# Two FFN layers with seven block products in place of eight, and the modulation vectors moved to the first layer

## The chip, the cores and the metric

The kernel runs on one core of one Trainium2 chip. The metric is the device time of one execution in microseconds (us); the time shown is the median of the runs.

## The reference

Two streams, 512 latent tokens and 256 context tokens of width 1024, pass through two layers. Each layer is a half FFN, a mixer, and a second half FFN. The mixer of the first layer (Fourier group and gated linear attention) is called even here, that of the second (short convolution and differential attention) odd. Every part has a normed input with a shift and a scale, and a gate on what it adds; these come from the conditioning vector of the stream.

```python
def _modulation(cond, w, b):
    m = jax.nn.silu(cond) @ w + b
    return jnp.split(m[..., None, :], N_MOD, axis=-1)

def _prenorm(h, gain, shift, scale):
    return _rmsnorm(h, gain) * (1.0 + scale) + shift

def _swiglu(h, w_in, w_out):
    g, u = jnp.split(h @ w_in, 2, axis=-1)
    return (jax.nn.silu(g) * u) @ w_out
...
        h = h + 0.5 * g1 * _swiglu(_prenorm(h, norm_ffn1[layer], sh1, sc1), ffn1_w_in[layer], ffn1_w_out[layer])
        hc = hc + 0.5 * cg1 * _swiglu(_prenorm(hc, norm_ffn1[layer], csh1, csc1), ffn1_w_in[layer], ffn1_w_out[layer])
```

The hidden width is 2816. There are nine modulation vectors for each layer and stream.

## The kernel before, in words

Activations lie transposed: 8 chunks of 128 features, each with the tokens along the free axis, and a token's normed input is h * gain * (1 + scale); the factor 1/rms of a token is multiplied in after the product (`scaled`, L305), and two extra columns hold the shifts of the two streams, so that one product gives tokens and shifts. To come near to float32, each operand is split into a high part (ScalarE's copy, `split_w` L164, `split` L145) and a low part (VectorE's difference, L165, L146), and each product is three matmuls (`mm3`, L248): high by high, high by low, low by high.

An FFN layer (`ffn`, L677) takes the 22 chunks of 128 hidden columns in four groups (6, 6, 6, 4). For a chunk it loads the weights of gate and up (1024 x 128 each, 512 KB) on SP's queue, splits them, and multiplies them with the two token halves, context (256, with the shifts 258 columns) and latent (512): 2 weights x 8 feature chunks x 3 matmuls, for each half. VectorE and ScalarE make the hidden chunk `hh`, `hl` from the sums. After a group, `out_phase` (L611) multiplies its hidden chunks with the output weights, 8 output chunks for each half, and adds the gated sum to the residual stream (`hlat`, `hctx`, L627). In front of the first layer come its own shift and scale.

The other modulation vectors are made on VectorE (`mod_tile`, L477): a tile of 128 outputs is loaded (`ada`, 512 KB on SP's queue) and for each stream one instruction multiplies it with the conditioning vector and adds up (`junk`, L484). A group of eight tiles is one vector. These tiles are dealt out evenly over the hidden chunks of a layer, from chunk 3 on: 48 tiles of two streams in the first FFN layer, 48 of two streams in the second, 32 of one stream in the third.

The order of instructions on each engine is set when the program is built, by a scheduler that takes the program's order as priority; every engine then takes its own list in that order. Pools of buffers decide when a tile can be written: 3 raw weights (`wraw`), 4 split weights (`wsp`), 7 hidden chunks, 4 modulation tiles in the first layer, 7 PSUM banks for sums (6 in the first layer).

## Time and profile before

| | us |
|---|---|
| device time, median of 3 runs | 2778.92 |
| lowest and highest run | 2778.41 and 2778.99 |
| span of the profiled execution, first to last instruction | 2776.5 |
| device time of the profiled execution itself | not recorded |
| TensorE busy | 2722.8 (98%) |
| VectorE busy | 1751.6 (63%) |
| ScalarE busy | 986.2 (36%) |
| GpSimd busy | 236.0 (9%) |

Busy time is the time in which at least one instruction of the engine runs; rows of one engine overlap, so that the sum of their lengths is more. DVE is VectorE, ACT ScalarE, PE TensorE, POOL GpSimd, SP the queue of the plain transfers. The layers follow one another: the first FFN layer to about 534 us, the even mixer to about 940, the second FFN layer to 1490, the third to 1985, the odd mixer to about 2390, then the last.

### The profile page before, as it was taken

The page shows a single profiled execution, that of the slowest core. Times are in us where ns is not written, and L with a number is a line of the kernel's source. Part 1 is how long each engine was busy: PE and PEld are TensorE (multiplying, and loading weights), DVE is VectorE, ACT ScalarE, POOL GpSimd, SP SyncE. Part 2 cuts the span into 40 slices and gives each one's busy share as a digit, 9 for nine tenths or more (in the row PEclk, how much of TensorE's full clock was granted, in tenths as well). Part 3 has the DMA queues.
Part 4 walks back from the last instruction along what each step waited for, and adds up shares of the span by engine and source line. Part 5 has one row for each costly group of instructions (what it writes and reads, how often), then busy time and mean ns, then how long its engine had stood idle before and what let it go on. Part 6 is the DMA issues. An engine that isn't in the chain of part 4 may idle for free.

```text
span 2776.5 us, 42228 instructions
## 1 busy us (share of the span) xinstructions
PE 2722.8 (98%) x17198; PEld 2425.7 (87%) x17198; DVE 1751.6 (63%) x3181; ACT 986.2 (36%) x1628; POOL 236.0 (9%) x231
## 2 busy tenths in 40 slices
PE   9999999999999999999999999999999999999998
PEld 7888888888888888888888888888888888999997
DVE  6647475678889764747566445454478888744545
ACT  4312121255544621212125212121256666522323
POOL 2000000030000200000002000000052223100002
PEclk9999999999999999999999999999999999999999
DMA  7324333312111132324332323233222212222221
GB/s 260 130 90 131 105 131 110 109 63 69 54 58 54 69 116 98 132 95 137 107 122 76 101 97 105 86 101 105 92 77 61 73 57 75 76 98 87 95 96 61
DMA packets 87554, 267.84 MB, mean 96 GB/s; under 512 B 10736, under 2 KB 18256, under 8 KB 87360
## 3 DMA queue, kind: packets, MB, share of 16 engines
q1 hardware_dynamic: 83248, 255.08, 27.4%
q0 software_dynamic: 3024, 9.01, 1.3%
q8 instruction: 136, 2.23, 0.3%
q10 hardware_dynamic: 1088, 1.05, 0.1%
q14 instruction: 58, 0.48, 0.1%
HBM read 255.14 MB, written 2.10 MB: 93 GB/s over the span
## 4 chain that ended last, share of the span: by engine, by line
PE 83%; DVE 11%; ACT 3%; issue 2%; DMA 1%; POOL 0%; SPq 0%; DVEq 0%; ACTq 0%; POOLq 0%
PE mm L170 81%; DVE al L602 1%; DVE mx L1245 1%; DVE gS L1046 1%; DVE hlat L627 1%; PE sc L170 1%; DVE wl L165 1%; ACT e L1247 1%; ACT wh L164 1%; PE n L170 0%; DVE hctx L627 0%; PE mm L177 0%; ACT ah L601 0%; DVE atl L146 0%; DVE e L1259 0%
## 5 line engine op out<-in xcount | busy, mean ns | idle before, releaser
L170 PE MATMUL mm<-ah,wh 128*128 128x258 f32 (+2 forms) x3536 | 1163.6, 329 | 7.4 <-DVE t L308 4.6
L170 PE MATMUL mm<-al,wh 128*128 128x258 f32 (+2 forms) x3536 | 1149.1, 325 | 0.0
L170 PE MATMUL mm<-ah,wl 128*128 128x258 f32 (+2 forms) x3536 | 1147.4, 324 | 1.6 <-DVE wl L165 1.6
L170 PEld LDWEIGHTS mm<-ah,wh 128*128 128x128 f32 x3536 | 669.2, 189 | 71.8 <-DVE t L308 4.2
L170 PEld LDWEIGHTS mm<-ah,wl 128*128 128x128 f32 x3536 | 669.2, 189 | 59.5 <-DVE wl L165 1.8
L170 PEld LDWEIGHTS mm<-al,wh 128*128 128x128 f32 x3536 | 670.2, 190 | 55.6 <-issue 1.4
L164 ACT ACTIVATE wh<-wr 128x1024 fp32r<-128x1024 f32 (+2 forms) x361 | 354.4, 982 | 934.5 <-PE mm L170 834.2
L170 PE MATMUL mm<-hh,wh 128*128 128x256 f32 (+1 forms) x1408 | 454.3, 323 | 0.0
L170 PE MATMUL mm<-hl,wh 128*128 128x256 f32 (+1 forms) x1408 | 453.3, 322 | 0.0
L170 PE MATMUL mm<-hh,wl 128*128 128x256 f32 (+1 forms) x1408 | 453.3, 322 | 0.0
L308 DVE TENSOR_TENSOR t<-mm,R 128x256 f32<-128x256 f32 (+2 forms) x376 | 195.1, 520 | 362.5 <-PE mm L170 362.1
L165 DVE TENSOR_TENSOR wl<-wr,wh 128x1024 fp32r<-128x1024 f32 (+2 forms) x325 | 371.1, 1142 | 47.8 <-ACT wh L164 43.5
L627 DVE SCALAR_TENSOR_TENSOR hlat<-mm,mod,hlat 128x512 f32<-128x512 f32 (+1 forms) x216 | 139.4, 649 | 277.2 <-PE mm L170 276.8
L170 PEld LDWEIGHTS mm<-hh,wl 128*128 128x128 f32 x1408 | 265.8, 189 | 23.5
L170 PEld LDWEIGHTS mm<-hl,wh 128*128 128x128 f32 x1408 | 264.5, 188 | 23.9
L170 PEld LDWEIGHTS mm<-hh,wh 128*128 128x128 f32 x1408 | 264.4, 188 | 23.9
L484 DVE SCALAR_TENSOR_TENSOR junk<-ada,cond 128x1024 bf16<-128x1024 f32 x224 | 273.8, 1222 | 2.8 <-DMA ada<-in_adaT_dram 2.3
L536 POOL TENSOR_TENSOR nacc<-nacc,nsq 128x256 f32<-128x256 f32 x47 | 39.5, 841 | 1973.9 <-ACT nsq L532 1945.2
L711 ACT ACTIVATE t<-t,c 128x256 f32<-128x256 f32 (+1 forms) x176 | 103.2, 586 | 247.4 <-DVE t L308 241.0
L145 ACT ACTIVATE hh<-t 128x256 fp32r<-128x256 f32 (+1 forms) x176 | 87.6, 498 | 280.9 <-DVE t L713 279.4
L713 DVE SCALAR_TENSOR_TENSOR t<-t,c,t 128x256 f32<-128x256 f32 (+1 forms) x176 | 102.7, 584 | 19.9 <-ACT t L711 4.7
L146 DVE TENSOR_TENSOR hl<-t,hh 128x256 fp32r<-128x256 f32 (+1 forms) x176 | 91.7, 521 | 35.2 <-ACT hh L145 35.0
(275 smaller groups left out, 2256.9 us busy)
## 6 DMA issues: line engine op xcount, KB each, us to landing
wr<-in_ffn_in_dram SPq DMA_DIRECT2D x176, 512.0 KB, 3.5
ada<-in_adaT_dram SPq DMA_DIRECT2D x128, 512.0 KB, 3.4
wr<-in_ffn_out_dram SPq DMA_DIRECT2D x96, 384.0 KB, 3.1
wr<-in_odd_w_dram SPq DMA_DIRECT2D x24, 512.0 KB, 3.5
wr<-in_even_w_dram SPq DMA_DIRECT2D x21, 512.0 KB, 3.5
wn<-in_ada_dram SPq DMA_DIRECT2D x16, 512.0 KB, 5.2
wr<-in_ffn_out_dram SPq DMA_DIRECT2D x16, 512.0 KB, 3.6
wr<-in_mix_out_dram SPq DMA_DIRECT2D x16, 256.0 KB, 2.6
```

The costliest lines, as they stand in the source:

```text
L145: self.nc.scalar.activation(hi, src, AF.Copy)
L146: self.nc.vector.tensor_tensor(lo, src, hi.bitcast(F32), op=ALU.subtract)
L164: self.nc.scalar.activation(hi, rv, AF.Copy)
L165: self.wl_engine.tensor_tensor(lo, rv, hi.bitcast(F32), op=ALU.subtract)
L170: i = self.nc.tensor.matmul(*a, **k)
L308: self.nc.vector.tensor_tensor(dst, ps, self.R[:ps.shape[0], hf[0]:hf[1]], op=ALU.mult)
L484: nc.vector.scalar_tensor_tensor(junk, w, 1.0, self.cond[:, s, :], op0=ALU.mult, op1=ALU.mult, accum_out=self.mods[l][:, s, n:n + 1]))
L536: self.acc_engine.tensor_tensor(acc[:, :w], acc[:, :w], sq[:, :w], op=ALU.add)
L602: nc.vector.scalar_tensor_tensor(lo[:, a], self.hv(k, s0, s1), G, hi[:, a].bitcast(F32), op0=ALU.mult, op1=ALU.subtract)
L627: nc.vector.scalar_tensor_tensor(hv, ps[:, s0 - t0:s1 - t0], gate, hv, op0=ALU.mult, op1=ALU.add)
L711: nc.scalar.activation(sg, sg, AF.Silu, bias=c[0][:, st:st + 1])
L713: nc.vector.scalar_tensor_tensor(sg, su, c[1][:, st:st + 1], sg, op0=ALU.add, op1=ALU.mult)
```

## The change

In the second and third FFN layer, chunks 2 to 21 are made by `ffn_fast`. A chunk's in-projection is seen as a 2 x 2 block product: the weights by gate and up and by the two halves of the features, the activations by the two halves of the features and of 772 columns (768 tokens and four columns of shifts), 386 each. Strassen's scheme in Winograd's form replaces the eight block products by seven, with sums of weight blocks and of activation blocks as operands, each product of 4 feature chunks x 3 matmuls x 386 columns.

- `sums_of_acts` makes the activation sums once in a layer: ScalarE writes unsplit activations into two buffers (`sg`), VectorE combines them, and they are split.
- The weight sums are made in part by transfers: SP loads a block of 256 KB into a buffer `sg`, and a transfer on GpSimd's queue adds the other block to it (`half_sum`, `SUM`). VectorE adds the rest (`prep`).
- The products of a chunk share PSUM banks; ScalarE copies partial sums out (`p1`, `p3`, `p5`), VectorE combines (`p6`, `p2`, `p7`, `p4`). TensorE takes the products of these layers in the order of the program.
- The groups are 2, 4, 4, 4, 4 and 4 chunks; 4 buffers for hidden chunks in place of 7.
- Modulation vectors: 96 tiles of two streams and 24 of one are computed in the first FFN layer (216 instructions, before 96), none in the second and third, and one vector (8 tiles of one stream) in the last; they are dealt out over chunks and over the units of the output phases (`pace`).

```diff
+    def sums_of_acts(self, l, gsh, gsc, tp):
+        nc = self.nc
+        TA, T3 = [], []
+        for kp in range(4):
+            b = []
+            for k in (kp, kp + 4):
+                x = self.sg.tile([P, 1024], F32, tag="sg", name=self.nm("bt"))[:, :TOK + 4]
+                for c0, c1, st in self.segs(0, TOK):
+                    nc.scalar.activation(x[:, c0:c1], self.hv(k, c0, c1), AF.Copy,
+                                         scale=self.mods[l][:, st, 8 * gsc + k:8 * gsc + k + 1])
+                S = self.mods[l][:, 0:2, 8 * gsh + k].unsqueeze(1).to_broadcast([P, 2, 2])
+                nc.scalar.activation(x[:, TOK:].rearrange("p (a b) -> p a b", b=2), S, AF.Copy)
+                b += [x[:, :HALF], x[:, HALF:]]
+            t = self.tmpt(TOK + 4)
+            t1, t2 = t[:, :HALF], t[:, HALF:]
+            nc.vector.tensor_tensor(t1, b[0], b[1], op=ALU.subtract)
+            nc.vector.scalar_tensor_tensor(t2, t1, -1.0, b[3], op0=ALU.mult, op1=ALU.subtract)
+            TA.append(tuple(tp.tile([P, TOK + 4], F32R, name=self.nm(n)) for n in ("tah", "tal")))
+            self.split(*TA[-1], t)
+            u = self.tmpt(TOK + 4)
+            t3, t4 = u[:, :HALF], u[:, HALF:]
+            nc.vector.tensor_tensor(t3, b[3], b[1], op=ALU.subtract)
+            nc.vector.scalar_tensor_tensor(t4, t2, -1.0, b[2], op0=ALU.mult, op1=ALU.subtract)
+            T3.append(tuple(tp.tile([P, HALF], F32R, name=self.nm(n)) for n in ("t3h", "t3l")))
+            self.split(*T3[-1], t3)
+            self.split(*(x[:, HALF:] for x in self.A[kp]), t4)
...
+    def ffn_fast(self, l, w_in, w_out, gate, gsh, gsc, halves, last):
+        nc, a = self.nc, self.a
+        win = a[w_in][l]
+        hid = self.hidden(l, w_in, [0, 1], halves)
+        with ExitStack() as es:
+            tp = es.enter_context(self.tc.tile_pool(name=self.nm("tp"), bufs=1))
+            rhs = self.sums_of_acts(l, gsh, gsc, tp)
+            self.run(self.out_phase(l, gate, w_out, 0, hid, halves, None))
+            end = FAST_GROUPS[-1][-1]
+            R1, R2 = self.R[:, :HALF], self.R[:, HALF:]
+            W, X, Y, G, U, sgs = {}, {}, {}, {}, {}, {}
+            hid = []
+            group = list(FAST_GROUPS)
+            def half_sum(j):
+                t = sgs[j] = self.sg.tile([P, 2, 512], F32, tag="sg", name=self.nm("sg"))
+                if j >= 2:
+                    SUM(t[:, 0, :], win[j][:, :512], win[NJ + j][:, :512])
+                if j < end:
+                    SUM(t[:, 1, :], win[NJ + j + 1][:, :512], win[NJ + j + 1][:, 512:])
+            def SUM(out, x, y):
+                nc.sync.dma_start(out, x)
+                nc.gpsimd.dma_start(out, y, accum_op=ALU.add)
+            def prep(j):
+                if j <= end:
+                    r = self.load_raw(win[j], KD)
+                    w1 = self.split_w(r, KD)
+                    s = sgs[j - 1][:, 1, :]
+                    nc.vector.tensor_tensor(r[:, :512], r[:, :512], s, op=ALU.add)
+                    nc.vector.tensor_tensor(r[:, 512:], r[:, 512:], r[:, :512], op=ALU.add)
+                    w2 = self.split_w(r, KD)
+                    W[j, 1], W[j, 2], W[j, 6], W[j, 3] = (w1, 0), (w1, 4), (w2, 0), (w2, 4)
+                if j - 1 >= 2:
+                    W[j - 1, 4] = self.load_w(win[NJ + j - 1][:, 512:], 4), 0
+                if j <= end:
+                    half_sum(j)
+                    n = KD if j < end else 4
+                    w3 = self.split_w(sgs[j].rearrange("p a b -> p (a b)")[:, :n * P], n)
+                    W[j, 7], W[j + 1, 5] = (w3, 0), (w3, 4)
+            def product(ps, j, i, start=True):
+                (hi, lo), o = W.pop((j, i))
+                self.pin = True
+                for k in range(4):
+                    self.mm3(ps, (hi[:, o + k, :], lo[:, o + k, :]), rhs[i][k], start and k == 0, k == 3, not start)
+                self.pin = False
+            def p5(j):
+                Y[j] = self.mmt(0)[:, :HALF]
+                U[j] = self.tmpt(TOK + 4)
+                product(Y[j], j, 5)
+                with hip():
+                    nc.scalar.activation(U[j][:, HALF:], Y[j], AF.Copy)
...
+            def p6(j):
+                product(X[j], j, 6, False)
+                g = G[j][:, HALF:]
+                with hip():
+                    nc.vector.tensor_tensor(g, X[j], g, op=ALU.add)
+            def p2(j):
+                z = self.mmt(0)[:, :HALF]
+                product(z, j, 2)
+                g = G[j]
+                with hip():
+                    nc.vector.tensor_tensor(g[:, :HALF], z, g[:, :HALF], op=ALU.add)
+                nc.vector.tensor_tensor(g, g, self.R, op=ALU.mult)
+                for t0, t1, st in self.segs(0, TOK):
+                    nc.scalar.activation(g[:, t0:t1], g[:, t0:t1], AF.Silu, bias=g[:, TOK + st:TOK + st + 1])
...
+            def p4(j):
+                product(X[j], j, 4, False)
+                g, u = G.pop(j), U.pop(j)
+                with hip():
+                    nc.vector.scalar_tensor_tensor(u[:, :HALF], X.pop(j), -1.0, R1, op0=ALU.mult, op1=ALU.mult)
+                for t0, t1, st in self.segs(0, TOK):
+                    nc.vector.scalar_tensor_tensor(g[:, t0:t1], u[:, t0:t1], u[:, TOK + st:TOK + st + 1], g[:, t0:t1],
+                                                   op0=ALU.add, op1=ALU.mult)
+                h = (self.hidp.tile([P, TOK], F32R, tag="hh", name=self.nm("hh")),
+                     self.hidp.tile([P, TOK], F32R, tag="hl", name=self.nm("hl")))
+                self.split(*h, g[:, :TOK])
+                hid.append(h)
...
+            hip = lambda: self.tc.high_priority(offset=HIP)
+            sgs[1] = None
+            half_sum(1)
+            w3 = self.split_w(sgs[1][:, 1, :], 4)
+            W[2, 5] = w3, 0
+            p5(2)
+            for j in range(2, end + 1):
+                prep(j)
+                p1(j)
+                p3(j)
+                if j > 2:
+                    p4(j - 1)
+                p6(j)
+                p2(j)
+                if group and j - 1 == group[0][-1]:
+                    out()
+                if j < end:
+                    p5(j + 1)
+                p7(j)
+            prep(end + 1)
+            p4(end)
+            out()
+        total = 9 * KD if len(mods) == KD else sum(3 * KD * len(g) for g in FFN_GROUPS) + sum(3 * KD * len(g) for g in FFN_GROUPS[:-1]) - 9 * KD
+        self.left, self.gone = list(mods), 0
+        def pace(cost):
+            self.gone += cost
+            n = len(mods) - int(len(mods) * max(0, 1 - self.gone / total))
+            while self.left and len(mods) - len(self.left) < n:
+                self.left.pop(0)()
...
+                if batch[-1] > 2:
+                    pace(3 * KD)
...
+            for m in self.out_phase(l, gate, w_out, grp[0], hid, halves, last if final else None):
+                if m == 0 and not final:
+                    pace(3 * len(grp) / len(halves))
...
+            if fast:
+                self.hidp = pool("hidp", 4)
+                self.tmpw = TOK + 4
+                self.tmp = pool("f_tmp", 5)
+                self.sg = pool("sgp", 2)
+                fn()
+                self.tmpw = 512
+                return
...
-                     self.mod_steps([(0, g, 2) for g in (G1, SCM, SHM, GM, SC2, SH2)]), norm_to(0, SHM, SCM), ws)
+                     self.mod_steps([(0, g, 2) for g in (G1, SCM, SHM, GM, SC2, SH2, G2)]
+                                    + [(1, g, 2) for g in (SC1, SH1, G1, SCM, SHM)]
+                                    + [(1, g, 1) for g in (GM, SC2, SH2)]), norm_to(0, SHM, SCM), ws)
...
-        self.ffn_scope(lambda: self.ffn(
-            0, "ffn2_in", "ffn2_out", G2, H,
-            self.mod_steps([(0, G2, 2)] + [(1, g, 2) for g in (SC1, SH1, G1, SCM, SHM)]), norm_to(1, SH1, SC1)))
+        self.ffn_scope(lambda: self.ffn_fast(0, "ffn2_in", "ffn2_out", G2, SH2, SC2, H, norm_to(1, SH1, SC1, scol=TOK)), fast=True)
...
-        self.ffn_scope(lambda: self.ffn(1, "ffn2_in", "ffn2_out", G2, HL, [], Final(self)))
+        self.ffn_scope(lambda: self.ffn(1, "ffn2_in", "ffn2_out", G2, HL, self.mod_steps([(1, G2, 1)]), Final(self)))
```

The order that the build sets moves as follows. First VectorE in the first FFN layer, at the start of the first output phase; `junk` are the modulation instructions, `hctx` and `hlat` the gated sums that free PSUM, `wl` the low part of a weight. Before:

```order
L627 SCALAR_TENSOR_TENSOR hlat<-mm_1474,mod_86,hlat 128x512
L627 SCALAR_TENSOR_TENSOR hctx<-mm_1454,mod_86,hctx 128x256
L627 SCALAR_TENSOR_TENSOR hctx<-mm_1500,mod_86,hctx 128x256
L627 SCALAR_TENSOR_TENSOR hlat<-mm_1520,mod_86,hlat 128x512
L165 TENSOR_TENSOR wl_1681<-wr_1678,wh_1680 128x768
L627 SCALAR_TENSOR_TENSOR hctx<-mm_1546,mod_86,hctx 128x256
L627 SCALAR_TENSOR_TENSOR hlat<-mm_1566,mod_86,hlat 128x512
L165 TENSOR_TENSOR wl_1727<-wr_1724,wh_1726 128x768
L627 SCALAR_TENSOR_TENSOR hctx<-mm_1592,mod_86,hctx 128x256
L627 SCALAR_TENSOR_TENSOR hlat<-mm_1612,mod_86,hlat 128x512
L165 TENSOR_TENSOR wl_1773<-wr_1770,wh_1772 128x768
```

With the change:

```order
L492 SCALAR_TENSOR_TENSOR junk_1450,mod_86<-ada_1448,cond_109 128x1024
L639 SCALAR_TENSOR_TENSOR hctx<-mm_1466,mod_86,hctx 128x256
L492 SCALAR_TENSOR_TENSOR junk_1452,mod_86<-ada_1448,cond_109 128x1024
L639 SCALAR_TENSOR_TENSOR hlat<-mm_1492,mod_86,hlat 128x512
L492 SCALAR_TENSOR_TENSOR junk_1456,mod_86<-ada_1454,cond_109 128x1024
L639 SCALAR_TENSOR_TENSOR hctx<-mm_1530,mod_86,hctx 128x256
L492 SCALAR_TENSOR_TENSOR junk_1458,mod_86<-ada_1454,cond_109 128x1024
L171 TENSOR_TENSOR wl_1711<-wr_1708,wh_1710 128x768
L492 SCALAR_TENSOR_TENSOR junk_1488,mod_86<-ada_1486,cond_109 128x1024
L639 SCALAR_TENSOR_TENSOR hlat<-mm_1556,mod_86,hlat 128x512
L492 SCALAR_TENSOR_TENSOR junk_1490,mod_86<-ada_1486,cond_109 128x1024
```

Between the gated sums, which stood beside weight splits alone, there now stand one or two modulation instructions each.

Second VectorE in the second FFN layer, around the last in-projection of chunks 0 and 1; `bt` are the unsplit activations, `tah`, `tal`, `t3h`, `t3l` the split sums, `hctx` the first gated sum of the output phase. With the change:

```order
L739 TENSOR_TENSOR t_9470<-bt_9462 128x386
L716 SCALAR_TENSOR_TENSOR t_9451<-t_9452,c_9333,t_9451 128x512
L740 SCALAR_TENSOR_TENSOR t_9470<-t_9470,bt_9466 128x386
L745 TENSOR_TENSOR t_9477<-bt_9466,bt_9462 128x386
L152 TENSOR_TENSOR hl_9208<-t_9451,hh_9207 128x512
L152 TENSOR_TENSOR tal_9474<-t_9470,tah_9473 128x772
L746 SCALAR_TENSOR_TENSOR t_9477<-t_9470,bt_9466 128x386
L152 TENSOR_TENSOR t3l_9481<-t_9477,t3h_9480 128x386
L739 TENSOR_TENSOR t_9494<-bt_9486 128x386
L152 TENSOR_TENSOR al_8857<-t_9477,ah_8856 128x386
L639 SCALAR_TENSOR_TENSOR hctx<-mm_9564,mod_86,hctx 128x256
```

None of the sums stood there before; they come beside and behind the last in-projection's results (`t_9451`, `hl_9208`), and the first gated sum stands behind the first pair of chunks.

Third VectorE in the middle of the second FFN layer, most of one period; `sg` is a weight sum, `wr` a raw weight, `mm` a product's bank, `R` is 1/rms. With the change:

```order
L835 TENSOR_TENSOR t_12341<-mm_12340,t_12341 128x386
L152 TENSOR_TENSOR hl_12384<-t_12208,hh_12383 128x768
L793 TENSOR_TENSOR wr_12446<-wr_12446,sg_12331 128x512
L842 TENSOR_TENSOR t_12341<-mm_12400,t_12341 128x386
L794 TENSOR_TENSOR wr_12446<-wr_12446 128x512
L843 TENSOR_TENSOR t_12341<-t_12341,R_8872 128x772
L171 TENSOR_TENSOR wl_12455<-wr_12446,wh_12454 128x1024
L851 TENSOR_TENSOR t_12285<-mm_12340,t_12285 128x386
L171 TENSOR_TENSOR wl_12461<-wr_12458,wh_12460 128x512
L852 SCALAR_TENSOR_TENSOR t_12285<-t_12285,R_8872 128x386
L171 TENSOR_TENSOR wl_12470<-sg_12464,wh_12469 128x1024
L860 SCALAR_TENSOR_TENSOR t_12341<-t_12285,t_12341 128x256
```

Before, a chunk had two splits of 1024 columns and the instructions on its gate and up sums and its hidden chunk; the combination of products, the sums on weights and the further splits are new.

## Rows read from the trace of the kernel before

**Rows 1.** The page: busy time, share and instructions of each engine.

```profile
PE 2722.8 (98%) x17198; PEld 2425.7 (87%) x17198; DVE 1751.6 (63%) x3181; ACT 986.2 (36%) x1628; POOL 236.0 (9%) x231
```

**Rows 2.** Windows view, four FFN layers: stretch, length, busy (instructions), clock, DMA share, GB/s.

```profile
104.00:534.00 430.00, 430.00 (x2453) 375.68 (x2452) 261.60 (x461) 92.41 (x124) 0.00 (x0) 1.00 0.35 116
940.00:1490.00 550.00, 550.00 (x3118) 479.51 (x3117) 338.75 (x596) 147.52 (x212) 14.21 (x12) 1.00 0.33 111
1490.00:1985.00 495.00, 495.00 (x2829) 432.82 (x2828) 230.86 (x386) 119.77 (x160) 2.62 (x2) 1.00 0.29 95
2390.00:2776.00 386.00, 373.36 (x3111) 372.35 (x3110) 193.97 (x368) 120.81 (x187) 13.98 (x18) 0.99 0.27 88
```

**Rows 3.** Waits view, TensorE: waited for, us in total, times, longest.

```profile
PE sc L170 <- ACT e L1247: 6.2, 9, 1.5
```

**Rows 4.** Timeline, TensorE, in-projection of layer 2: start, length, instruction.

```profile
1252.23 0.28 PE L170 MATMUL mm<-ah,wh 128*128 128x258 f32 x1
...
1258.06 0.40 PE L170 MATMUL mm<-ah,wh 128*128 128x512 f32 x1
...
1269.17 0.28 PE L170 MATMUL mm<-ah,wh 128*128 128x258 f32 x1
```

**Rows 5.** Timeline, TensorE, output phase of layer 2.

```profile
1204.14 0.28 PE L170 MATMUL mm<-hh,wh 128*128 128x256 f32 x1
...
1206.18 0.39 PE L170 MATMUL mm<-hh,wh 128*128 128x512 f32 x1
...
1210.38 0.28 PE L170 MATMUL mm<-hh,wh 128*128 128x256 f32 x1
```

**Rows 6.** Timeline and groups by shape, TensorE, scores of the odd mixer.

```profile
2214.61 0.86 PE L170 MATMUL sc<-T,Q 128*128 128x384 f32 x4
...
L170 PE MATMUL sc<-T,Q 128*128 128x384 f32 x192 | 42.9, 345 | 6.7 <-ACT e L1247 6.2 <-DMA Q<-Q 0.5
```

**Rows 7.** Groups by shape, VectorE, 95 to 540 us, first FFN layer.

```profile
L484 DVE SCALAR_TENSOR_TENSOR junk<-ada,cond 128x1024 bf16<-128x1024 f32 x86 | 104.9, 1220 | 0.2
L165 DVE TENSOR_TENSOR wl<-wr,wh 128x1024 fp32r<-128x1024 f32 x35 | 42.7, 1221 | 2.8 <-ACT wh L164 1.5
L308 DVE TENSOR_TENSOR t<-mm,R 128x512 f32<-128x512 f32 x36 | 24.8, 689 | 80.9 <-PE mm L170 80.9
...
L627 DVE SCALAR_TENSOR_TENSOR hctx<-mm,mod,hctx 128x256 f32<-128x256 f32 x24 | 11.5, 482 | 3.5 <-PE mm L170 3.5
```

**Rows 8.** Timeline, VectorE, a modulation instruction and what follows.

```profile
221.79 1.22 DVE L484 SCALAR_TENSOR_TENSOR junk<-ada,cond 128x1024 bf16<-128x1024 f32 x1
...
222.94 0.15 DVE L286 COPY c<-mm 128x2 f32<-128x2 f32 x1
```

**Rows 9.** Waits view, VectorE, first FFN layer.

```profile
DVE hlat L627 <- PE mm L170: 72.3, 21, 3.7
...
DVE hl L146 <- ACT hh L145: 5.2, 11, 0.7
```

**Rows 10.** Groups by shape, ScalarE, 1000 to 1480 us, second FFN layer.

```profile
L164 ACT ACTIVATE wh<-wr 128x1024 fp32r<-128x1024 f32 x39 | 41.4, 1061 | 128.1 <-PE mm L170 116.5 <-issue 11.6
...
L145 ACT ACTIVATE hh<-t 128x512 fp32r<-128x512 f32 x19 | 12.0, 633 | 19.6 <-DVE t L713 19.6
```

**Rows 11.** DMA issues: queue, count, size, median us to landing.

```profile
wr<-in_mix_out_dram SPq DMA_DIRECT2D x16, 256.0 KB, 2.6
...
Q<-Q POOLq DMA_DIRECT2D x24, 128.0 KB, 2.5
...
k<-k POOLq DMA_DIRECT2D x6, 192.0 KB, 3.9
hctx<-in_hT_dram SPq DMA_DIRECT2D x1, 1024.0 KB, 9.1
```

**Rows 12.** Tile view of junk, its waits; windows view of the odd mixer.

```profile
  DMA ada<-in_adaT_dram: 2.3, 5
...
2080.00:2310.00 230.00, 218.27 (x1402) 197.69 (x1401) 192.10 (x366) 144.80 (x279) 64.46 (x52) 1.00 0.22 65
```

148 lines of the change are left out of this document (88 added, 60 removed).

## The prediction, made before the changed kernel ran

> **What bounds the kernel now.** I read the page's busy times first: TensorE is busy for 2722.8 of 2776.5 us [rows 1]. An average can hide stages with other limits, so I then cut out the four FFN layers with the windows view [rows 2]. In the second and third (940 to 1490 and 1490 to 1985 us) TensorE is busy in every microsecond, at a granted clock of 1.00 (its upper level, 2.4 GHz), with VectorE busy for 339 of 550 and 231 of 495 us. The first layer reads the same, with VectorE at 262 of 430. So in the FFN layers only TensorE's instructions count: what shortens their list is worth its full time as long as nothing else becomes late. TensorE's longest total of waits on anything, over the whole kernel, is 6.2 us [rows 3], and it lies in the odd mixer.
>
> A busy matmul row is longer than what the matmul costs, since rows overlap. I therefore use the pitch from start to start. One chunk of hidden columns in layer 2 shows 48 matmuls of 258 columns from 1252.23 to 1258.06, which is 121.5 ns each, and 48 of 512 columns from there to 1269.17, 231.5 ns each [rows 4]. A chunk costs 16.94 us. In the output phase 18 matmuls of 256 columns take 2.04 us (113.3 ns) and 18 of 512 take 4.20 us (233.3 ns) [rows 5].
>
> **Fewer products in layers 2 and 3.** For 20 of 22 chunks in each of the two layers, 96 matmuls become 7 x 4 x 3 = 84 of 386 columns. No row has 386 columns. On the line between 258 and 512 columns it is 176.9 ns; between the output phase's 256 and 512 it is 174.3. Four matmuls of 384 columns in the odd mixer span 0.86 us, the last of them 0.345 long, so 172 ns each [rows 6]. I take 175, between the three. A chunk is then 84 x 0.175 = 14.70 us, 2.24 less, and 40 chunks save **90 us**; the ends 172 and 177 give 100 and 83. The Trainium skill's page "TensorE: Matmul & The Clock Gate" (section "Back-to-back issue gap") gives columns / 2.4 + 2.5 ns, by which 512, 258 and 386 columns would take an estimated 216, 110 and 163 ns and the saving would be 77 us; the 231.5 ns of rows 4 does not agree with it.
>
> Does the new chunk keep TensorE fed? By the order of each engine a period of 14.7 us holds the products 5, 7, 1, 3, 4, 6, 2. Between a product and the next one into the same bank lie two others, 4.2 us, for ScalarE's copy or VectorE's sum of 386 columns (some 0.5 us by the widths of rows 7 and 10). VectorE's 15 instructions of a period come to about 10.6 us: 3.5 weight splits of 1.14 (1.22 less some 0.08 by which rows overlap [rows 8]), two sums of 512 columns (1.2), and the eight combinations (5.4). ScalarE's come to 7.3 (3.5 splits of 1.06 and six smaller ones) [rows 7, 10]. Following the order by hand, the tightest weight (products 6 and 3, which wait for two sums on VectorE) is there 2.8 us early; in front of an output phase the last hidden chunk's low part is ready 1.1 us before its first use. I cost the chunks at no stall, and the ten output phases and two layer ends at 2 us together (0 to 8). The modulation vectors that leave these layers (96 and 32 VectorE instructions) gain nothing, as VectorE had idle time there [rows 2].
>
> **The start of each of the two layers.** This is new waiting. The first product (5) of chunk 2 needs the sums of all activations and one weight sum, and only the output phase of chunks 0 and 1 covers them: 8 x 6 x (0.1133 + 0.2333) = 16.6 us. The sums share two buffers with the weight sums. Behind the last in-projection they run one chunk pair after the other: ScalarE makes two inputs (some 2.5 us), VectorE two sums of 0.5, ScalarE the splits (2 us, partly beside). The first pair is through 3.5 us after TensorE's last product, the three others take 5 us each, so the buffer is free after 18.6 us. Then come a plain transfer of 256 KB (2.6), the accumulating one, and a half split on ScalarE and on VectorE with their hops (1.5) [rows 7, 10, 11]. The trace has no accumulating transfer: transfers on POOL's queue land in 2.5 and 3.9 us, the slowest of all in 9.1 [rows 11]. I take 4, at the upper POOL row, as it reads what it adds to. That gives 26.7 us against 16.6: **10 us late, twice, 20 us**. Bounds are 4 each (pairs overlapping to 3.5 us, 2.5 us of landing) and 15 each (9.1 us of landing). The Trainium skill's page "SBUF — State Buffer" (section "SBUF: two separate sides") warns that a DMA from GpSimd's queue waits while VectorE holds the port they share, an estimated 1.2 us a start, 2.4 in the sum; here Q<-Q landed in 2.5 us with VectorE busy for 192 of 230 us [rows 11, 12], so I add nothing.
>
> **More modulation in the first layer.** VectorE there gets 216 of these instructions in place of 96. One occupies it for 1.15 us, start 221.79 to the next at 222.94 [rows 8]; its long transfers were awaited for only 2.3 us in all 224 cases [rows 12]. From the first output phase to the end of the third, TensorE needs 3 x 49.9 + 12 x 16.94 = 353 us. In the changed order 180 of the instructions stand there, 207 us. The rest of VectorE's work runs at (261.6 - 86 x 1.15) / 430 = 0.378 per us [rows 2, 7, 8], 134 us in 353. Together 341 us, **97%**: there is no overload, but no slack either, and VectorE takes its list in order. I counted one crossing: from the first modulation instruction behind the first group's last in-projection to the low part of chunk 8's second weight there are 85.7 us of VectorE work, begun 3 us into the phase, so ready at 88.7, while TensorE wants it at 49.9 + 2 x 16.94 + 3.2 = 87.0. That is a wait of 1.7 us, and the lists allow some more of that kind. I take seven, **12 us** (0, as 341 fits in 353, to 25, where half of VectorE's 72 us of waits for `hlat` sums [rows 9] returns less the slack of 12). In the last FFN layer 8 such instructions, 9 us, lie under VectorE's idle time (194 of 386 us busy [rows 2]): nothing.
>
> **Sum.** -90 + 20 + 12 + 2 = -56 us. The profiled span of 2776.5 becomes 2720.5. Its own device time is not given; the median of the three runs, 2778.92, is 2.4 above the span, and I carry that along: **2723 us**.
>
> **The rivals.** (a) VectorE becomes the bound of the first layer. For it: 97%, in order, with weight splits behind modulation instructions. Against: before, its waits on ScalarE in this layer were 5.2 us and the rest were for TensorE, which is slack [rows 9]. If a third of the 180 instructions (60) cost TensorE 0.8 us each, the layer loses 48 in place of 12: 2759 us. (b) Both edges stay under cover: 8 in place of 20, 0 in place of 12 and 2 saved: 2697 us. For it: the lower bounds above. Against: the chain through two shared buffers is longer than its cover by 10. (c) Slower: the accumulating transfer. Two buffers rotate; a buffer is free at the end of a period and its sum is wanted one period and 4.7 us later, 19.4 us. Plain transfer plus landing beyond that lengthens the period by the same amount. The gain of 56, 1.4 us per chunk, is gone when the two take 20.8 us, so when the accumulating one lands in 18 us; at 20 us the time is 2723 + 40 x 3.2 = 2851 us. Against: 18 is nearly five times the slower POOL row [rows 11]. For: nothing here accumulates, so its rate is not known. That the products are not really fewer is no rival: the order has 3360 matmuls of 386 columns.
>
> **How the numbers follow.** Forecast 0.70, (a) 0.17, (b) 0.08, (c) 0.05. About 0.2%, 5.5 us, is what a measurement here can tell from no change. The bounds of the terms taken together (83 to 100 saved; 8 to 30, 0 to 25 and 0 to 8 given back) leave a gain in every case but (c) and the far end of (a): faster 0.93, within 0.2% 0.02, slower 0.05. The range 2692 to 2757 takes in the forecast's likely spread, (b) and half of (a).
>
> **What would show it.** In the profile after: 386-column matmuls at a pitch of 172 to 177 ns; periods of 14.7 us with TensorE at 100% in the middle of layers 2 and 3; one gap or stretched output phase of some 10 us near the start of each, released by `wh`, `wl` or the sum transfer; small waits for `wl` or `t` in the first layer with VectorE near 97%. I am wrong if the pitch is above 185 ns, if TensorE waits in every period, if the accumulating transfer takes over 10 us, or if the first layer loses over 25 us.

## The result and the profile after

The changed kernel takes **2728.86 us** (median of 4 runs, 2726.38 to 2729.58); the kernel before, run beside it, 2778.95. The ratio is 0.9816, 95% interval 0.9802 to 0.9830: 50 us less. Forecast were 2723 us, a range of 2692 to 2757 and 0.93 for faster.

The page's first section, after, stands against [rows 1]:

```profile
PE 2662.0 (98%) x16718; PEld 2441.8 (90%) x16718; DVE 1965.1 (72%) x3415; ACT 1114.2 (41%) x1852; POOL 305.6 (11%) x313
```

TensorE has 480 matmuls and 61 us of busy time fewer, which is more than the 50 us that the span lost: TensorE now idles somewhere. VectorE has 213 us more. The windows view says where (columns as in [rows 2]): the first layer, the start of the second, the middles of the second and third.

```profile
100.00:500.00 400.00, 398.49 (x2272) 348.41 (x2271) 377.30 (x689) 83.95 (x111) 0.00 (x0) 1.00 0.62 198
970.00:998.60 28.60, 22.78 (x97) 17.45 (x96) 26.96 (x49) 16.09 (x34) 2.73 (x3) 0.82 0.28 65
1100.00:1500.00 400.00, 400.00 (x2265) 377.53 (x2264) 249.44 (x364) 160.13 (x240) 37.38 (x40) 1.00 0.34 91
1600.00:2000.00 400.00, 400.00 (x2272) 377.94 (x2271) 251.98 (x358) 146.61 (x218) 45.13 (x44) 1.00 0.36 96
```

In the middles TensorE is busy without a break at a granted clock of 1.00: the seven products are fed, and the next layer's activations come in time. One stretch has a hole and a lower clock, the start of the second layer; the third has the same at 1510 to 1530 us.

Where the 50 us lie between the stages, the tile view shows: first and last start of a product that opens the even mixer, and of the odd mixer's scores (the last two numbers before the shape). Before:

```profile
L170 PE MATMUL mm<-wh,zfh x12: 279/284/387, 624.5 to 645.2; 128*128 128x256 f32 x12
L170 PE MATMUL sc<-T,Q x192: 331/337/447, 2079.2 to 2354.0; 128*128 128x384 f32 x192
```

After:

```profile
L176 PE MATMUL mm<-wh,zfh x12: 279/284/386, 628.3 to 649.0; 128*128 128x256 f32 x12
L176 PE MATMUL sc<-T,Q x192: 330/337/522, 2029.0 to 2304.3; 128*128 128x384 f32 x192
```

The mixer opens 3.8 us later, the scores 50.2 us earlier, and the span ends 50.0 us earlier. So the first layer loses 3.8 us, the two fast layers gain 54, and what follows changes by nothing.

The pitch of the new products, from TensorE's timeline (start, length, instruction; 24 matmuls from the first row to the last):

```profile
1199.71 0.34 PE L176 MATMUL mm<-t3h,wh 128*128 128x386 f32 x1
...
1203.94 0.35 PE L176 MATMUL mm<-ah,wh 128*128 128x386 f32 x1
```

That is 176 ns. The period of a chunk, from ScalarE's timeline, is 14.83 us, or 176.6 ns for each of 84:

```profile
1129.91 0.85 ACT L151 ACTIVATE hh<-t 128x768 fp32r<-128x768 f32 x1 [0.50 <-DVE t L860]
1144.74 0.85 ACT L151 ACTIVATE hh<-t 128x768 fp32r<-128x768 f32 x1 [0.50 <-DVE t L860]
1159.58 0.85 ACT L151 ACTIVATE hh<-t 128x768 fp32r<-128x768 f32 x1 [0.50 <-DVE t L860]
```

Forty chunks save 40 x (16.94 - 14.83) = **84 us**. The Trainium skill's formula ("TensorE: Matmul & The Clock Gate", section "Back-to-back issue gap"), which the page gives for an isolated matmul, makes an estimated 163 ns; the 176 measured here, in a stream of matmuls and weight loads, does not agree with it.

**The start of layer 2.** The first row is where the first output phase begins, the second the first product of chunk 2:

```profile
969.91 0.28 PE L176 MATMUL mm<-hh,wh 128*128 128x256 f32 x1
...
998.62 0.34 PE L176 MATMUL mm<-tah,wh 128*128 128x386 f32 x1
```

28.7 us, where the phase by itself takes some 17 (8 x 6 x (0.118 + 0.233) = 16.9). VectorE in that stretch, grouped (count, busy us and mean ns, idle time ahead of it):

```profile
L639 DVE SCALAR_TENSOR_TENSOR hlat<-mm,mod,hlat 128x512 f32<-128x512 f32 x7 | 5.2, 743 | 0.0
L639 DVE SCALAR_TENSOR_TENSOR hctx<-mm,mod,hctx 128x256 f32<-128x256 f32 x8 | 3.8, 477 | 0.0
L152 DVE TENSOR_TENSOR tal<-t,tah 128x772 fp32r<-128x772 f32 x4 | 3.8, 953 | 0.0
L745 DVE TENSOR_TENSOR t<-bt,bt 128x386 f32<-128x386 f32 x4 | 2.2, 555 | 0.0
...
L739 DVE TENSOR_TENSOR t<-bt 128x386 f32<-128x386 f32 x4 | 2.2, 554 | 0.0
```

No idle time ahead of any of them: VectorE takes one after the other. The sums and splits of one pair take 3.7 us of VectorE (four sums and two half splits at a pitch of 0.47 us, one whole split of 0.87). The gated sums that free the output phase's PSUM banks stand between them, two in 4.75 us, where TensorE makes two such products in 2.1 us (6 x 0.118 + 6 x 0.233). The timeline of the same engine shows it, and its end:

```profile
980.43 0.56 DVE L739 TENSOR_TENSOR t<-bt 128x386 f32<-128x386 f32 x1
980.90 0.48 DVE L639 SCALAR_TENSOR_TENSOR hctx<-mm,mod,hctx 128x256 f32<-128x256 f32 x1
982.70 0.75 DVE L639 SCALAR_TENSOR_TENSOR hlat<-mm,mod,hlat 128x512 f32<-128x512 f32 x1
985.18 0.56 DVE L739 TENSOR_TENSOR t<-bt 128x386 f32<-128x386 f32 x1
...
993.08 0.68 DVE L171 TENSOR_TENSOR wl<-wr,wh 128x512 fp32r<-128x512 f32 x1
995.03 0.69 DVE L171 TENSOR_TENSOR wl<-sg,wh 128x512 fp32r<-128x512 f32 x1 [1.27 <-ACT wh L170]
```

The last weights of the output phase (`wl<-wr`) come only behind all these sums, at 993.1. The weight sum of chunk 2, on which the prediction put the delay, is split at 995.0 to 995.7, ahead of 998.6.

### The profile page after: what moved, and what is told of

It reads as the page before. It is cut to its first block, busy times and chain, and to the rows that moved or that the text cites. A ratio compares the mean times of both kernels' runs of the same rounds, so it can differ in the third digit from the quotient of the medians.

```text
span 2726.5 us, 42007 instructions
## 1 busy us (share of the span) xinstructions
PE 2662.0 (98%) x16718; PEld 2441.8 (90%) x16718; DVE 1965.1 (72%) x3415; ACT 1114.2 (41%) x1852; POOL 305.6 (11%) x313
## 4 chain that ended last, share of the span: by engine, by line
PE 82%; DVE 12%; ACT 3%; issue 2%; DMA 1%; SPq 0%; POOL 0%; DVEq 0%; ACTq 0%; POOLq 0%
PE mm L176 80%; DVE al L614 1%; DVE hlat L639 1%; DVE mx L1444 1%; DVE gS L1245 1%; PE sc L176 1%; DVE wl L171 1%; ACT wh L170 1%; ACT e L1446 1%; PE n L176 1%; PE mm L183 0%; DVE atl L152 0%; DVE hctx L639 0%; DVE ry L1354 0%; DVE e L1458 0%
## 5 line engine op out<-in xcount | busy, mean ns | idle before, releaser
L176 PE MATMUL mm<-ah,wh 128*128 128x258 f32 (+3 forms) x2896 | 947.3, 327 | 7.5 <-DVE t L315 4.0
L176 PE MATMUL mm<-ah,wl 128*128 128x258 f32 (+3 forms) x2896 | 930.8, 322 | 3.4 <-DVE wl L171 3.4
L176 PE MATMUL mm<-al,wh 128*128 128x258 f32 (+3 forms) x2896 | 932.3, 322 | 0.0
L176 PEld LDWEIGHTS mm<-ah,wh 128*128 128x128 f32 x2896 | 548.6, 189 | 43.5 <-DVE t L315 4.8
L176 PEld LDWEIGHTS mm<-ah,wl 128*128 128x128 f32 x2896 | 547.9, 189 | 34.6 <-DVE wl L171 5.0
L176 PEld LDWEIGHTS mm<-al,wh 128*128 128x128 f32 x2896 | 548.8, 190 | 27.5 <-issue 1.7
L315 DVE TENSOR_TENSOR t<-mm,R 128x256 f32<-128x256 f32 (+1 forms) x216 | 106.5, 494 | 103.5 <-PE mm L176 103.0
L785 POOL DMA_DIRECT2D sg<-in_ffn_in_dram x80 | 71.0, 1015 | 849.5 <-DVE hctx L639 356.1
L151 ACT ACTIVATE hh<-t 128x256 fp32r<-128x256 f32 (+2 forms) x136 | 79.6, 585 | 174.2 <-DVE t L716 151.0
L714 ACT ACTIVATE t<-t,c 128x256 f32<-128x256 f32 (+1 forms) x96 | 54.1, 563 | 136.5 <-DVE t L315 133.5
```

Of the source, the lines that this page charges most:

```text
L151: self.nc.scalar.activation(hi, src, AF.Copy)
L176: i = self.nc.tensor.matmul(*a, **k)
L315: self.nc.vector.tensor_tensor(dst, ps, self.R[:ps.shape[0], hf[0]:hf[1]], op=ALU.mult)
L714: nc.scalar.activation(sg, sg, AF.Silu, bias=c[0][:, st:st + 1])
L785: nc.gpsimd.dma_start(out, y, accum_op=ALU.add)
```

## The experiments

Two theories stood at first. **From the profile after:** at the start VectorE's own work is the bound; the first layer's 3.8 us are waits for VectorE. **The prediction's:** the chain of two shared buffers and the accumulating transfer is the bound; the first layer loses 12 us.

### The modulation alone

```diff
-self.ffn_scope(lambda: self.ffn_fast(0, "ffn2_in", ...), fast=True)
+self.ffn_scope(lambda: self.ffn(0, "ffn2_in", "ffn2_out", G2, H, [], norm_to(1, SH1, SC1)))
```

(the third layer likewise, and the norm ahead of them puts its shift columns where the kernel before has them; the call is shortened where it says `...`)

> Only the modulation half of the change: all 216 modulation instructions in the first layer, 8 in the last, layers 2 and 3 with eight block products as before. Theory (from the traces: the first mixer product stands 3.8 us later after the change than before, the last stages are unchanged): 3 to 5 us above the kernel before, 2783 us. The prediction's term of 12 us would give 2791 us; the rival that VectorE bounds the first layer (48 us) would give 2827 us. In layers 2 and 3 the instructions that left were under TensorE's work, so these layers should keep their length to within 0.5 us.

Measured: **2789.07 us**, ratio 1.0035 (1.0022 to 1.0048), 9.5 us slower than before. Neither theory fits. The tile view, as above:

```profile
L176 PE MATMUL mm<-wh,zfh x12: 279/284/385, 628.9 to 649.5; 128*128 128x256 f32 x12
L176 PE MATMUL sc<-T,Q x192: 331/337/522, 2089.4 to 2364.1; 128*128 128x384 f32 x192
```

Of 10.6 us in the span only 4.4 lie ahead of the even mixer; 5.8 lie between the mixer and the scores, in layers with the eight products of before and with less work on VectorE.

### Shorter output phases

```diff
-        for gi, grp in enumerate(FFN_GROUPS):
+        groups = [range(0, 2)] + FAST_GROUPS if self.short else FFN_GROUPS
+        for gi, grp in enumerate(groups):
```

> As the kernel with the modulation moved alone, but layers 2 and 3 with the output phases of the changed kernel (groups of 2, 4, 4, 4, 4, 4 hidden chunks in place of 6, 6, 6, 4). Same matmuls, more and shorter chains. Theory: a chain of 256 columns costs a fixed 0.19 us beside 103 ns a matmul (18 take 2.05 us, 12 take 1.43), so two more phases of 8 such chains a layer cost 2.9 us a layer, 5.9 us together: 2789 us, if the modulation alone gives 2783. Rival (the prediction, which gave the ten phases and two ends 2 us in all): 2783 to 2785 us.

(`self.short` is set in these two layers alone.) Measured: **2789.19 us**, no different from the modulation alone, where I had expected 5.9 us more. So a chain has no fixed cost that shows. But the 256-column matmuls are slow in both kernels: 18 take 2.12 to 2.13 us in place of the 2.04 of [rows 5]. It is not the length of the chain, and it is there in the first layer too. What differs is the address: the compiled kernel before places the hidden tiles `hh` and `hl` at multiples of 64 bytes (the first at 133888; the traces hold no addresses). The change widens the tile of R, a line that the cuts above leave out, and the hidden tiles of every layer move by 32 bytes (133920):

```diff
-                n.R = n.apool.tile([P, TOK], F32, tag="R", name=n.nm("R"))
+                n.R = n.apool.tile([P, TOK + 4], F32, tag="R", name=n.nm("R"))
```

### 32 bytes, taken out and put in

```diff
-        c = self.cpool.tile([P, 2], F32, tag="c", name=self.nm("c"), bufs=6)[:m]
+        c = self.cpool.tile([P, 2], F32, tag="c", name=self.nm("c"), bufs=5)[:m]
```

in the kernel with the modulation alone, and in the changed kernel; seven buffers in the kernel before. A buffer of c takes 32 bytes. All that is allocated behind c moves with the hidden tiles, the split sums (`tah`, `t3h`) too; the weights and the activations `ah`, `al` stay where they are.

> As the kernel with the modulation moved alone, every instruction in the same order, but one buffer fewer of the tiny tile c (5 in place of 6), so that every pool behind it starts 32 bytes earlier. In the kernel before the hidden tiles start at multiples of 64 bytes; since the activation and R tiles were widened from 770 and 768 to 772 columns they start 32 bytes past one, in every kernel of the change. Theory: that offset is what makes a 256-column matmul of the output phases cost 118.3 ns in place of 113.7, 528 of them in each of three layers, 7.3 us: this kernel comes out at 2782 us (2780 to 2783) with the pitch back at 113.7 ns. Rival: the pitch depends on something else (the number of live buffers, the neighbouring work): 2789 us, pitch 118 ns.

> The kernel before with nothing of the change but 32 bytes: one buffer more of the tiny tile c (7 in place of 6; one constant column moves into another tile to make room), so that the hidden tiles start 32 bytes past a multiple of 64 as they do in the changed kernel. Theory: the offset alone costs what its removal gave back, 8 to 9 us: 2788 us, with the 256-column matmuls of the output phases at 118 ns. Rival: the offset matters only together with the widened activation tiles: 2779 us.

> The changed kernel with 32 bytes taken out in front of the hidden tiles (five buffers of c), nothing else. Theory: 8 to 9 us less than the changed kernel, 2720 us (2718 to 2722): that is what the seven products and the moved modulation come to when the layout does not change by the way. Rival: the gain is in the stretched starts' shadow or goes to the 386-column matmuls, whose own tiles move too: 2727 us.

Measured: the modulation alone with the shift **2780.27 us**, ratio 1.0004 (0.9996 to 1.0013); the kernel before with the offset **2787.01 us**, 1.0029 (1.0019 to 1.0040); the changed kernel with the shift **2719.64 us**, 0.9786 (0.9773 to 0.9799). So 32 bytes are worth 8.8, 7.5 and 9.2 us. The output phase's timeline in the kernel before with the offset (18 matmuls of 256 columns from the first row to the second):

```profile
1035.83 0.28 PE L170 MATMUL mm<-hh,wh 128*128 128x256 f32 x1
...
1037.96 0.39 PE L170 MATMUL mm<-hh,wh 128*128 128x512 f32 x1
```

2.13 us, 118.3 ns each, against 113.3 in [rows 5]. In the changed kernel 12 take 1.42 us:

```profile
1069.15 0.28 PE L176 MATMUL mm<-hh,wh 128*128 128x256 f32 x1
...
1070.57 0.39 PE L176 MATMUL mm<-hh,wh 128*128 128x512 f32 x1
```

and with the shift 1.37, 114.2 ns each:

```profile
1070.79 0.28 PE L176 MATMUL mm<-hh,wh 128*128 128x256 f32 x1
...
1072.16 0.39 PE L176 MATMUL mm<-hh,wh 128*128 128x512 f32 x1
```

Three layers with 528 such matmuls each at 4.2 to 5.0 ns make 6.7 to 7.9 us. In the changed kernel the shift gave a little more: the period of a chunk, which holds 386-column matmuls alone, is 14.79 us in place of 14.83 (ScalarE's timeline), 1.6 us for 40 chunks.

```profile
1126.87 0.85 ACT L151 ACTIVATE hh<-t 128x768 fp32r<-128x768 f32 x1 [0.50 <-DVE t L860]
1141.66 0.85 ACT L151 ACTIVATE hh<-t 128x768 fp32r<-128x768 f32 x1 [0.50 <-DVE t L860]
```

Together 8.3 to 9.5, against 9.2 measured. The modulation, moved, costs 0.9 us in the median, which the interval does not tell from nothing.

### The sums of the activations earlier

The first two lines stand in `hidden`, behind each of its four steps; the next ones in `sums_of_acts`, the last in `ffn_fast`.

```diff
+            if between:
+                next(between, None)
...
-            t3, t4 = u[:, :HALF], u[:, HALF:]
+            t3 = u[:, :HALF]
+            t4 = self.hidp.tile([P, TOK], F32, tag=("hh", "hl")[kp % 2], name=self.nm("t4"))[:, :HALF]
...
-            self.split(*(x[:, HALF:] for x in self.A[kp]), t4)
+            yield
+        for kp in range(4):
+            self.split(*(x[:, HALF:] for x in self.A[kp]), T4[kp])
...
-            rhs = self.sums_of_acts(l, gsh, gsc, tp)
+            sums = self.sums_of_acts(l, gsh, gsc, tp)
+            hid = self.hidden(l, w_in, [0, 1], halves, between=sums)
+            self.run(sums)
```

> The changed kernel with the activation sums of a layer issued between the in-projections of chunks 0 and 1, one pair behind each of the four steps, in place of behind them; one sum of each pair waits in a hidden buffer that is free then and is split at the end. Same work, earlier. Theory: the 28.7 us from the last in-projection product to the first 386-column product come down to the output phase's own 17.7 us and TensorE does not idle there, so its clock does not fall either: 11 us a layer, 2707 us (2703 to 2712). Rival 1: the sums are in the way of the in-projections' evacuations on VectorE and ScalarE, half of the gain goes: 2718 us. Rival 2: the start was not what cost the 11 us: 2728 us. It does not tell VectorE's load from the chain of two buffers and transfers, since both end earlier.

Measured: **2705.34 us**, ratio 0.9734 (0.9721 to 0.9748), 23.5 less than the changed kernel. TensorE's timeline, the same two rows as above:

```profile
970.23 0.28 PE L176 MATMUL mm<-hh,wh 128*128 128x256 f32 x1
...
987.67 0.34 PE L176 MATMUL mm<-tah,wh 128*128 128x386 f32 x1
```

17.4 us in place of 28.7, and the windows view of the stretch has TensorE busy for 17.28 of 17.50 us at a clock of 1.00:

```profile
970.20:987.70 17.50, 17.28 (x98) 14.75 (x97) 16.66 (x30) 4.55 (x8) 2.73 (x3) 1.00 0.59 141
```

By the device times a start had cost 11.8 us (23.5 / 2), in the trace of the first 28.7 - 17.4 = 11.3.

### Without the accumulating transfer at the start

```diff
-            half_sum(1)
+            t = sgs[1] = self.sg.tile([P, 2, 512], F32, tag="sg", name=self.nm("sg"))
+            nc.sync.dma_start(t[:, 1, :], win[NJ + 2][:, :512])
```

> The changed kernel without the accumulating transfer of the first weight sum of each layer (chunk 2's product 5 gets half of its sum; the output is not the reference's). Theory: at the start VectorE is the bound (busy without a break from 970.1 to 993.7 us, 26.96 of 28.6 us), and its sums hold up the gated sums that free the PSUM banks of the output phase; the weight, ready at 995.7, comes 3 us before TensorE wants it at 998.6. So nothing is gained: 2727 to 2729 us. Rival (the prediction's chain: two shared buffers, plain transfer, accumulating transfer, split): the accumulating transfer takes 3.9 us of the chain, 990.5 to 994.4, so 3.9 us a layer are gained: 2721 us.

Measured: **2729.94 us**, ratio 0.9821 (0.9808 to 0.9835): nothing gained (1 us above the range that I gave). ScalarE's timeline shows that the edit did shorten the chain; the same row stood at 994.37 in the changed kernel:

```profile
991.33 0.63 ACT L170 ACTIVATE wh<-sg 128x512 fp32r<-128x512 f32 x1 [1.65 <-DMA sg<-in_ffn_in_dram]
```

The first product of chunk 2 comes no earlier for it (1000.5 against 998.6; the phase takes 29.2 us, from 971.3 on). So the accumulating transfer does not bound the start. With the run before it and the timeline of VectorE, which has no pause from 970 to 993.7 us, this leaves VectorE's load. The sums of the pairs, the front part of the prediction's chain, are themselves a part of that load.

### TensorE kept busy at the start

```diff
+                        if warm and m + i < 6:
+                            ps = self.psn()
+                            for _ in range(warm):
+                                self.mm(ps[:, :256], acts[0][0][:, :P], acts[0][0][:, :256], start=True, stop=True)
```

> The changed kernel with 60 matmuls of 256 columns more in the first output phase of layers 2 and 3 (five ahead of each of the first twelve chains, results not used), 7 us of TensorE work a layer in the gaps where TensorE waits for banks, so that its clock does not fall there. Theory: VectorE is the bound up to 993.7 us, and only the 4.9 us behind it ran on TensorE's own time at a granted clock of 0.62 to 0.70: 0 to 1.5 us a layer, 2726 to 2729 us, with the clock of that stretch at 0.9 or more. Rival: the lower clock is what stretches the start (20 us at a mean of 0.74, some 4 us a layer): 2721 us.

Measured: **2727.72 us**, ratio 0.9815 (0.9801 to 0.9828), about 1 us less than without. The windows view of 980 to 1000 us, changed kernel:

```profile
980.00:1000.00 20.00, 14.33 (x52) 10.72 (x51) 18.30 (x34) 8.18 (x17) 2.73 (x3) 0.74 0.40 93
```

and with the filling:

```profile
980.00:1000.00 20.00, 18.09 (x109) 15.89 (x108) 18.29 (x35) 9.15 (x20) 2.76 (x3) 1.00 0.41 93
```

The clock of 0.74 is gone, VectorE's 18.3 of 20 us are not. The phase, which begins at 971.01 here, ends at 997.23: 26.2 us in place of 28.7.

```profile
971.01 0.28 PE L176 MATMUL mm<-hh,wh 128*128 128x256 f32 x1
...
997.23 0.34 PE L176 MATMUL mm<-tah,wh 128*128 128x386 f32 x1
```

So the lower clock stretched the phase by some 2.5 us, but more than half of that does not reach the total: the products behind it then wait 0.8 us for `wh` and 0.6 for `wl` (waits view, 997 to 1010 us), where the changed kernel waits 0.3. The weights, made on ScalarE and VectorE, stand close behind as the next bound. The lower clock was in the main a consequence of waiting, not the price.

### More modulation in the first layer

```diff
-                                    + [(1, g, 1) for g in (GM, SC2, SH2)]),
+                                    + [(1, g, 2) for g in (GM, SC2, SH2)]),
```

> The changed kernel with 24 modulation instructions more in the first layer (second stream of three vectors that use one; results not used), 240 in place of 216. VectorE is busy there for 377 of the 400 us from 100 to 500 us, so 23 us are idle, and some 20 of the 24 instructions, 23 us, fall into this stretch. Theory: the idle time is used up and TensorE begins to wait for weight splits behind modulation instructions: 2735 us (2731 to 2745), waits for wl in the first layer of several us where there were 1.5. Rival 1: all of it still fits, 2729 to 2730 us. Rival 2 (the prediction's case of a VectorE-bound layer): each crossing costs 0.8 us and the time goes to 2750 us or more.

Measured: **2732.84 us** (2730.39 to 2734.69), ratio 0.9832 (0.9819 to 0.9846), 4.0 more than the changed kernel: at the lower end of the expected range, but the place I gave was wrong. VectorE's busy time from 100 to 500 us is the same, 377.04; the 24 came last in the list and fell between 500 and 600 us, where VectorE had 28 us idle. So the run does not test the full stretch. It shows only that another 28 us of VectorE work there (24 x 1.15) cost 4 us by the medians. The trace shows half of it: one wait more of TensorE for `wl`, 1.8 us at 546.6, and the even mixer opens 2.2 us later (630.5).

### Two and three accumulating transfers for each sum

```diff
                 nc.gpsimd.dma_start(out, y, accum_op=ALU.add)
+                nc.gpsimd.dma_start(out, y, accum_op=ALU.add)
```

The added line stands once for two transfers, twice for three.

> The changed kernel with each accumulating transfer of a weight sum issued three times (the sum is of other weights, so the output is not the reference's). Theory: in the steady state a sum has 19.4 us from the free buffer to its use, and plain transfer and three accumulating ones take about 3 + 3 x 3.9 = 15 us, so the periods of 14.83 us stay as they are; only at the two starts some 8 us more of the chain stand against 3 us that it has in hand, 5 us each: 2738 us (2733 to 2742). Rival (the prediction's slow case, a landing of 5.5 us for each): 3 + 16.5 = 19.5 us, just over the 19.4 us, periods begin to lengthen: 2745 us or more.

> The changed kernel with each accumulating transfer issued twice (three times gave 2783.7 us; the sums are of other weights). In that trace POOL's own queue sets the pace: it issues the accumulating transfers of one sum after the other, and the steps of three stand 16.3 and 17.0 us apart, above the period of 14.83 us. Theory: POOL's step for two is then some 11 to 12 us, under the period, so the periods stay at 14.83 us and only the starts pay, where a further 4 us stand against 3 us in hand: 2731 us (2728 to 2735). Rival: the cost is proportional to the accumulating transfers (55 us for two more, 27 for one): 2756 us.

Measured: three **2783.71 us**, ratio 1.0017 (1.0008 to 1.0026); two **2742.70 us**, 0.9868 (0.9851 to 0.9884). Both came out above what I expected. With three, POOL's timeline (issue of a transfer, what it waited for) shows each further transfer wait for the landing of an earlier one, and a pause ahead of the next step:

```profile
1240.08 1.77 POOL L785 DMA_DIRECT2D sg<-in_ffn_in_dram  x2 [17.00 <-ACT t L847]
1244.88 0.87 POOL L786 DMA_DIRECT2D sg<-in_ffn_in_dram  x1 [3.03 <-DMA sg<-in_ffn_in_dram]
...
1252.53 0.87 POOL L787 DMA_DIRECT2D sg<-in_ffn_in_dram  x1 [1.58 <-DMA sg<-in_ffn_in_dram]
1256.43 1.78 POOL L785 DMA_DIRECT2D sg<-in_ffn_in_dram  x2 [3.03 <-DVE t L853]
```

The steps stand 16.3 and 17.0 us apart, over the 14.83 of a period, but POOL's own queue, on which I had put it, does not set the pace: it is idle for 3.0 us ahead of the step at 1256.43, for which SP issued the plain transfers at 1251.31; these landed 4.6 to 4.7 us after their issue. It is the whole chain of a sum that is too long, from the plain transfer (SP's timeline) to the split on ScalarE:

```profile
1236.46 0.80 SPq L784 DMA_DIRECT2D sg<-in_ffn_in_dram  x2
1251.31 0.82 SPq L784 DMA_DIRECT2D sg<-in_ffn_in_dram  x2
...
1257.88 1.06 ACT L170 ACTIVATE wh<-sg 128x1024 fp32r<-128x1024 f32 x1 [2.52 <-DMA sg<-in_ffn_in_dram]
1276.64 1.06 ACT L170 ACTIVATE wh<-sg 128x1024 fp32r<-128x1024 f32 x1 [6.44 <-DMA sg<-in_ffn_in_dram]
```

These are 21.4 and 25.3 us; in the changed kernel the same two points lie 18.8 us apart (1025.11 and 1043.90) and the split waits for nothing. The sum then comes late, and a period of 16.5 us or more stands in eight of the ten groups. That is the rival that I had set against the theory: a chain over 19.4 us.

With two, the periods inside the groups stay at 14.83, as expected, but for the first of a layer (14.01) and the last two, which are no other in the changed kernel; the starts pay instead, where I had allowed 1 us each. There the weight is now the bound (timeline, TensorE):

```profile
1004.19 0.69 PE L176 MATMUL mm<-tah,wh 128*128 128x386 f32 x1 [3.49 <-ACT wh L170]
```

at 1004.2 in place of 998.6, and from the last hidden chunk of one fast layer to the first of the next are 125.6 in place of 117.8 us. Why a second transfer costs some 8 us and not 4, the DMA view of the issues at 992 and at 996 us shows, the first and the second transfer of that sum:

```profile
sg<-in_ffn_in_dram POOLq DMA_DIRECT2D x1, 256.0 KB, 3.7
sg<-in_ffn_in_dram POOLq DMA_DIRECT2D x1, 256.0 KB, 7.2
```

The second is issued at 996.23, 4.0 us behind the first, and lands 7.2 us later where the first took 3.7: 7.5 us more. Transfers of two other sums are under way on the same queue then; that they slow it was not tested.

### Both together

The early sums and five buffers of c, the two edits shown above.

> The changed kernel with the sums issued early and with the same shift of 32 bytes. Theory: the same 528 matmuls in each of the three layers with 256-column halves come back by 4.6 ns each: 7 us less than with the sums early alone (2705.3), 2698 us (2696 to 2700). Rival: no change from the shift, 2705 us; or the 386-column matmuls, whose tiles move from one 32-byte offset to the other, lose what the others gain.

Measured: **2696.40 us** (2694.95 to 2697.52), ratio 0.9702 (0.9688 to 0.9715). It beats both kernels, by 83 and 32 us. The sum closes to half a microsecond: 2779.4 before, less 84.3 for the products, plus 0.9 for the modulation, is 2696.0.

## Why the prediction was right, and where not

The direction and the size were right, 2723 against 2728.9, but two of its terms were off in opposite directions, one had the wrong cause, and one effect was not in it.

- **In-projections, -90: right mechanism, -84 measured.** The pitch is 176.6 ns, not 175. The line between 258 and 512 columns of the same tiles had given 176.9; I took a value between it and two rows of other tiles, which pulled it down. The bounds, 83 to 100, held it. Chunks at no stall was right: TensorE 400.00 of 400 us in both middles.
- **The start, +10 each: right size (11.3 to 11.8), wrong step.** The failed step is "VectorE two sums of 0.5": I costed the sums as links of a chain and not as load. A pair has four sums and three splits, 3.7 us of VectorE, 14.8 for the four; 16 gated sums of 0.40 and 0.66 us are 8.5 more. With the weight splits and the last hidden chunk VectorE is busy for 27 of 28.6 us, against a cover of 17. The chain I gave was timed well (26.7 us from the last product against 995.7 - 969.9 = 25.8), but its tail of transfers and splits ran beside the bound, as the run without the transfer shows. That the size came out right is luck in this sense: a chain of 26.7 us and a load of 27 happen to be alike.
- **First layer, +12: wrong, nothing measurable.** VectorE was near 97% as forecast (94% over 400 us, 99% from 300 to 400), but TensorE waited for `wl` twice, 1.5 us in all. I had counted one crossing of 1.7 us, at the second weight of chunk 8, and then taken seven. At chunk 8 (from 219.2 us) TensorE waits for nothing; the two waits, 1.24 and 0.27 us, end at 239.3 and 391.9, in the fourth chunk behind an output phase and not in the third. So the size of one was near and its place was not; the other six had no row. The rest of the 3.8 us is the 32 bytes: 528 matmuls at 4.2 to 5.0 ns are 2.2 to 2.6 us.
- **Ends and phases, +2, and last layer, 0:** nothing found; the span ends as much earlier as the scores start.
- **Not foreseen, +9:** the 32 bytes. The wider tile of R stands in the change; no step of mine asked what lies behind it.
- **The accumulating transfer**, taken at 4, lands in 5.5 us in the median (a plain one into the same tile in 3.1), inside the bounds:

```profile
sg<-in_ffn_in_dram SPq DMA_DIRECT2D x80, 256.0 KB, 3.1
sg<-in_ffn_in_dram POOLq DMA_DIRECT2D x80, 256.0 KB, 5.5
```

Of the rivals, (a) did not come; a layer near 97% on an engine in order was not bound by it here. What the prediction put against it was read too low, VectorE's waits on ScalarE there being 7.3 us in all and not 5.2 (1.6 for `wl` and 0.5 for `t` beside the 5.2 for `hl`); nothing hangs on it. (b) had the first layer right and the starts wrong; with the early sums they fall even below its 4 us each (17.4 us against the phase's own 16.9). (c) did not come with one transfer; with three its rule held, and its point of decision, 19.4 us, was near the 18.8 that the changed kernel leaves a sum.

The sum, by what the runs gave: -84.3 + 23.5 + 9.2 + 1.5 (the two waits) = -50.1; measured -50.1. Such closeness is chance, as the kernel before differs by 0.6 us between the sets of runs from which the terms come (2778.95 to 2779.56).

## What to carry to other kernels

Cost a new step twice, as a chain of links and as load on each engine it uses, against the cover it stands under; the second is the one that bound here. When work must finish before a point, look first for an idle stretch ahead of it: 23 us came back by issuing the same instructions half a stage earlier. After any change of a tile's width, compare the pitch of an instruction that was not touched; where it moved, a layout effect lies beside the one you study.

## What was not expected of the hardware

- Moving operands of 256 columns in 4-byte elements cost TensorE 118.3 ns when their tiles start 32 bytes past a multiple of 64 and 113.3 to 114.2 when at one, with the same list of matmuls; the 512-column ones between them take 233 ns either way. The Trainium skill ("SBUF — State Buffer", section "Operand start alignment") allows any multiple of the element size and says that its runs timed nothing; the difference is measured here. Why it is so is open, and the runs do not tell whether it is the offset in 64 bytes as such: in the kernel before, the in-projections' 258-column matmuls take 120 to 123 ns with tiles at either offset, and the last layer's 256-column ones 117 to 120 ns with hidden tiles at multiples of 64.
- TensorE's granted clock fell from 1.00 to 0.74 in the mean of 20 us in which it was busy for 14.33, part of the time at its lower level (1.2 GHz), and was 1.00 again from 1000 us on. By the run that filled the gaps it cost that output phase some 2.5 us and the whole about 1 us.
- An accumulating transfer of 256 KB takes POOL 0.88 us to issue and lands in 5.5 us in the median, where a plain one into the same tile takes 3.1. In this program the next into the same tile waits on POOL until it has landed; the second at the start took 7.2 us where the first took 3.7.
